# Mixture of experts: order by token count, half-width slots for four experts, 2 MB weight transfers

## The chip, the cores and the metric

The kernel runs on one core of a Trainium2 chip. The metric is the time of one execution on the device, in microseconds (us); lower is better. In the rows PE is the matrix engine (TensorE), PEld its weight loads, DVE the vector engine, ACT the scalar engine, POOL the GpSimd engine and SP the engine that issues the weight transfers; SPq is its queue. 1 MB is 1,048,576 bytes throughout.

## The reference, cut to what matters

The network has two blocks over 256 tokens of width 1024 in fp32. The changed part is the mixture of experts that ends the first block:

```python
def moe_swiglu(h, w_router, w_gate_up, w_down):
    t = h.reshape(-1, D)                                    # 256 x 1024
    logits = (t @ w_router).astype(F32)                     # 8 experts
    top_val, top_idx = lax.top_k(logits, TOP_K)             # 2 of 8
    top_w = jax.nn.softmax(top_val, axis=-1)
    combine = jnp.sum(jax.nn.one_hot(top_idx, N_EXPERTS, dtype=F32) * top_w[..., None], axis=1)
    for e in range(N_EXPERTS):
        gt, up = jnp.split(t @ w_gate_up[e], 2, axis=-1)    # 1024 x 2*3584
        y = (jax.nn.silu(gt) * up) @ w_down[e]              # 3584 x 1024
        out = out + combine[:, e:e + 1].astype(t.dtype) * y
```

With the inputs of the measurement the eight experts get 55, 74, 53, 86, 71, 54, 55 and 64 of the 512 (token, expert) pairs. An expert's weights are 42 MB, all experts' 336 MB.

## The kernel before

**Products.** An fp32 product is made of parts that the matrix engine takes at full rate: x = xH + xL and w = wH + wL, and `mm3` (L185, matmuls at L187 to L189) adds wH xH, wL xH and wH xL. Weights come from DRAM into a ring of raw slots of 1 MB (DMA at L172, on SP's queue), ACT copies the high part wH (L182) and DVE subtracts to get wL (L183), 1024 columns of 128 partitions, half a slot, at a time.

**Routing.** `route` computes logits, ranks and `place`, each token's place among its expert's tokens. The count of the fullest expert goes to a register (`values_load`, L977); if it is over 128 a branch (L872) runs all experts again on the tokens beyond 128.

**Experts.** `experts` takes experts 0 to 7 in this order, each with 128 slots. For a pair of experts `pair` gathers the tokens of both by a product with a one-hot matrix (L998) and makes the parts hH and hL. Each expert has 7 groups of 512 hidden columns. `up` makes the gate and up products of a group (8 blocks of channels, each an `mm3` of a 128x128 stationary block of tokens and 512 weight columns, result `gu`), then silu on ACT (L1086), the product with up on DVE (L1087), four transposes on PE (L192) and the parts aH (ACT) and aL (DVE). `down` adds the group before it into two accumulators `acc` (2 halves x 4 blocks of `mm3`). So an expert has 7 x 2 x 8 x 3 + 7 x 2 x 4 x 3 = 504 of these matmuls. After the last group `scatter` adds the slots' results to the tokens (L1134 to L1136). `first_gates` makes the gates of expert 0's first group for all tokens while the routing still runs.

**Rings.** During the experts `more_raw` lengthens the ring to 12 slots: the 5 slots that all stages share, 5 new ones and 2 in the pair of tiles (`hp`) that the stage before has used for its operand parts. The whole program lies in one `weights` context (`tile_stages`), so the next stage, `mixer_2`, loads into the same 5 slots.

Of the kernel before, what the change touches and what calls it, by code (L numbers as in the profile page):

```python
# [30 lines left out]
RAW = 5  # L31
LEVELS = (64, 32, 16, 8, 4, 2, 1)
# [53 lines left out]
class Net:  # L86
    def __init__(self, ctx, tc, A, out):
# [3 lines left out]
        self.grain = 1024  # columns of weights that are split in one operation  # L91
# [4 lines left out]
        self.turn = 0  # of hp, the one last taken from  # L96
# [32 lines left out]
    def more_raw(self, bufs, more):  # L129
        """Lengthens the ring of bufs raw weights, by more new ones and the two tiles of hp that aren't in use."""  # L130
        was, spare = self.ring, self.hp[1 - self.turn]
        with self.tc.tile_pool(name="more", bufs=more) as pool:
            more_ = lambda n: pool.tile([128, n], F32, name="raw", tag="raw")
            spare_ = [lambda n, tag=tag: spare.tile([128, n], F32, name="raw", tag=tag) for tag in ("hH", "hL")]
            turns = itertools.cycle([more_] * more + [was[0]] * bufs + spare_)
            self.ring = (lambda n: next(turns)(n)), *was[1:]
            yield
        self.ring = was
# [12 lines left out]
    def row(self, ap, pool, name, eng=None, **k):  # L151
        """One row of DRAM on all partitions."""
# [5 lines left out]
    def col(self, ap, pool, name, eng=None):  # L158
        """A row of 1024 in DRAM as [128, chunk]."""
# [4 lines left out]
    def unit(self, srcs, a, b):  # L164
        """The weights of a ring's slot, [128, a, b], and their two exact parts. srcs: (index of the view, DRAM AP)."""
# [14 lines left out]
    def parts(self, H, L, src):  # L180
        """src = H + L, each of 12 significant bits."""
# [12 lines left out]
    def rstd(self, ss, n, width):  # L194
        """ss [128, width] sums of squares -> 1/sqrt(mean + eps)."""
# [5 lines left out]
    def power(self, x):  # L201
        """1/sqrt(x) of x [128, few]."""
# [4 lines left out]
    def squares(self, x, ss, junk=None):  # L207
        """The sum of squares of each row of x [128, <=512] to ss [128, 1]; on VectorE with junk."""
# [6 lines left out]
    def to_T(self, src, t, u, dH, dL, psum):  # L215
        """Half u of the channels of src [128 tokens, 1024] -> parts of the transpose in dH/dL[:, :, t*128:]."""
# [1333 lines left out]
```

## Time and profile before

| | before |
|---|---|
| three runs, median (lowest to highest) | 1872.41 us (1871.2 to 1872.74) |
| profiled execution, span from its first to its last instruction | 1871.3 us |
| PE busy | 1811.4 us, 97% |
| DVE busy | 1477.5 us, 79% |
| ACT busy | 1230.4 us, 66% |
| moved by DMA | 511.36 MB (of 10^6 bytes) |

The profiled execution's only time is its span; it lies 1.1 us under the median of the runs. Busy time is a sum over stages with different limits, so the experts' stage, from about 516 to 1528 us, has to be read by itself.

### The profile page before, as it was taken

To read this page: it belongs to the slowest core of one execution; us is meant where nothing else is said; L and a number is where in the kernel's file an instruction comes from. 1 tells how busy PE (TensorE), PEld (TensorE's weight loads), DVE (VectorE), ACT (ScalarE), POOL (GpSimd) and SP (SyncE) were. 2 spreads that over 40 slices of the span, in tenths; PEclk is the share of its full clock that TensorE was granted. 3 is DMA by queue.
4 is the path that set the end of the run, shared out by engine and by line. 5 is a ranking of instruction groups with operands and counts; after the bars stand their busy time and mean duration, and the time that the engine had idled before them with its cause. 6 is when DMAs were issued, how large, how long until landed. Compare 5 with 4: busy or idle time off the path is not lost. (4 is left out here: it accounts for less than half of the span.)

```text
span 1871.3 us, 23420 instructions
## 1 busy us (share of the span) xinstructions
PE 1811.4 (97%) x8504; PEld 1455.9 (78%) x8504; DVE 1477.5 (79%) x1826; ACT 1230.4 (66%) x1768; POOL 73.1 (4%) x113
## 2 busy tenths in 40 slices
PE   7999999999999999999999999999999979989997
PEld 5767787788778888788787887887887857778886
DVE  4767888676789998898988989988898876575555
ACT  5665444575678777777777777777777766565443
POOL 2002000120100000000000000000000010000001
PEclk9999999999999999999999999999999989999999
DMA  8536899643579999899999999998999935345551
GB/s 250 172 94 232 311 335 328 223 149 113 208 275 364 372 356 370 324 351 365 341 372 346 338 361 356 355 371 301 360 376 341 345 122 169 129 158 191 180 180 45
DMA packets 226299, 511.36 MB, mean 273 GB/s; under 512 B 11301, under 2 KB 37013, under 8 KB 223104
## 3 DMA queue, kind: packets, MB, share of 16 engines
q1 hardware_dynamic: 221872, 501.84, 75.6%
q0 software_dynamic: 2832, 7.09, 1.5%
q8 instruction: 69, 1.13, 0.2%
q10 hardware_dynamic: 1472, 0.86, 0.2%
q14 instruction: 54, 0.44, 0.1%
HBM read 507.10 MB, written 2.65 MB: 272 GB/s over the span
## 5 line engine op out<-in xcount | busy, mean ns | idle before, releaser
L183 DVE TENSOR_TENSOR wL<-raw,wH 128x1024 fp32r<-128x1024 f32 (+1 forms) x1001 | 1072.0, 1115 | 209.3 <-issue 125.7
L182 ACT ACTIVATE wH<-raw 128x1024 fp32r<-128x1024 f32 (+1 forms) x1001 | 912.3, 969 | 242.5 <-PE acc L189 70.1
L187 PE MATMUL gu<-wH,hH 128*128 128x512 f32 x1192 | 467.5, 392 | 2.3 <-ACT hH L1000 2.3
L188 PE MATMUL gu<-wL,hH 128*128 128x512 f32 x1192 | 466.3, 391 | 3.1 <-DVE wL L183 3.0
L189 PE MATMUL gu<-wH,hL 128*128 128x512 f32 x1192 | 465.5, 391 | 0.0
L188 PEld LDWEIGHTS gu<-wL,hH 128*128 128x128 f32 x1192 | 224.4, 188 | 56.4 <-DVE wL L183 5.7
L189 PE MATMUL acc<-wH,aL 128*128 128x512 f32 x664 | 265.5, 400 | 0.0
L187 PEld LDWEIGHTS gu<-wH,hH 128*128 128x128 f32 x1192 | 224.4, 188 | 51.0 <-ACT hH L1000 3.7
L188 PE MATMUL acc<-wL,aH 128*128 128x512 f32 x664 | 263.4, 397 | 0.0
L189 PEld LDWEIGHTS gu<-wH,hL 128*128 128x128 f32 x1192 | 224.2, 188 | 46.6 <-issue 1.1
L187 PE MATMUL acc<-wH,aH 128*128 128x512 f32 x664 | 257.3, 402 | 0.0
L187 PE MATMUL mm<-wH,hH 128*128 128x512 f32 (+1 forms) x384 | 151.7, 396 | 0.8 <-ACT hH L1478 0.5
L188 PE MATMUL mm<-wL,hH 128*128 128x512 f32 (+1 forms) x384 | 150.2, 391 | 0.0
L188 PEld LDWEIGHTS acc<-wL,aH 128*128 128x128 f32 x664 | 124.8, 188 | 32.2 <-DVE wL L183 4.1
L189 PE MATMUL mm<-wH,hL 128*128 128x512 f32 (+1 forms) x384 | 149.4, 390 | 0.0
L187 PEld LDWEIGHTS acc<-wH,aH 128*128 128x128 f32 x664 | 124.9, 188 | 26.5 <-issue 0.5
L189 PEld LDWEIGHTS acc<-wH,aL 128*128 128x128 f32 x664 | 124.8, 188 | 26.5 <-issue 0.5
L182 ACT ACTIVATE aH<-tp 128x512 fp32r<-128x512 f32 (+1 forms) x94 | 51.1, 545 | 120.3 <-PE tp L192 120.2
L187 PEld LDWEIGHTS mm<-wH,hH 128*128 128x128 f32 x384 | 73.2, 191 | 15.3 <-issue 1.7
L188 PEld LDWEIGHTS mm<-wL,hH 128*128 128x128 f32 x384 | 73.2, 191 | 14.5 <-issue 2.7
L189 PEld LDWEIGHTS mm<-wH,hL 128*128 128x128 f32 x384 | 73.2, 191 | 13.5 <-issue 1.7
L1087 DVE SCALAR_TENSOR_TENSOR act<-gu,r_slot,act 128x512 f32<-128x512 f32 x56 | 42.0, 749 | 49.2 <-PE gu L189 49.2
(434 smaller groups left out, 1428.5 us busy)
## 6 DMA issues: line engine op xcount, KB each, us to landing
raw<-in_moe_w_gate_up_dram SPq DMA_DIRECT2D x224, 1024.0 KB, 7.3
raw<-in_moe_w_down_dram SPq DMA_DIRECT2D x112, 1024.0 KB, 6.4
raw<-in_w_ff_dram SPq DMA_DIRECT2D x32, 1024.0 KB, 5.0
raw<-in_w_ada_dram SPq DMA_DIRECT2D x24, 1024.0 KB, 4.9
raw<-in_dense_w_gate_up_dram SPq DMA_DIRECT2D x44, 512.0 KB, 5.2
raw<-in_b_w_in_dram SPq DMA_DIRECT2D x12, 1024.0 KB, 5.1
raw<-in_w_in_dram SPq DMA_DIRECT2D x12, 1024.0 KB, 5.5
raw<-in_dense_w_down_dram SPq DMA_DIRECT2D x11, 1024.0 KB, 5.1
```

What stands on the lines that cost most here:

```text
L182: self.high = self.nc.scalar.activation(H, src, AF.Copy)
L183: self.low = self.nc.vector.tensor_tensor(L, src, H.bitcast(F32), op=OP.subtract)
L187: mm(ps, xH, wH, start=start, stop=False)
L188: mm(ps, xH, wL, start=False, stop=False)
L189: mm(ps, xL, wH, start=False, stop=stop)
L1087: nc.vector.scalar_tensor_tensor(a, ps[1], r, a, op0=OP.mult, op1=OP.mult)
```

## The change

**Order.** After the counts are known, `order` (a function inside `route`) ranks the experts by their count on DVE, expert 0 first whatever it has. SP reads the seven numbers of the others and the fullest count into registers; the weights of turns 1 to 7 are then addressed by register.

**Slots.** Turns 0 to 3 have 128 slots as before. Turns 4 to 7 have 64, and their stationary operand holds the 64 high columns beside the 64 low ones. One 128x512 matmul with wH makes wH xH in the upper half of the result and wH xL in the lower; a second with wL uses the 64 high columns alone (`product`). That is 2 matmuls for 3. The halves of the gate are added by copying the result (ACT, `halves`) and an fp32 product with `fold`, which sums slots i and i+64. The up product is not folded: the four transposes become fp32 products with `fold`, which add the halves as they transpose. The one-hot is written twice, so that the scatter adds the halves.

**Weights.** A transfer fills a slot of 2 MB: 4 blocks of channels x 1024 columns for gate and up (runs of 4 KB in DRAM, before 2 KB), and 16 KB per partition in one run for down (before 4 KB). `wH` and `wL` are made 2048 columns at a time. Groups are taken in steps (0), (1,2), (3,4), (5,6). The ring has 4 slots of 2 MB and the spare `hp` pair (2 x 1 MB), 10 MB in all, before 12 MB.

**Gathers** are made for turns (0), (1,2), (3) and (4 to 7), each ahead of the last `down` of the turn before it. Activations are issued behind the first piece of the `down` before them.

**Fallback.** The branch is taken when a count is over 128, or over 64 in turns 4 to 7. Ranked, the counts above are 55 (expert 0), 86, 74, 71 and 64, 55, 54, 53.

**Contexts.** The experts no longer lie in the shared `weights` context; `mixer_2` and `mlp` open one of their own behind it.

```diff
...
+    def wide_weights(self, slots, high, low, size, spare=None):
...
+            n = 4096 if slots else size
+            slot = lambda: a.tile([128, n], F32, name="raw", tag="raw")
+            turns = [[slot] * (4096 // n)] * max(1, slots)
+            if spare is not None:
+                turns.append([lambda tag=tag: spare.tile([128, size], F32, name="raw", tag=tag) for tag in ("hH", "hL")])
...
+        for make in next(turns):
+            raw = make()
+            n = raw.shape[-1]
+            nc.sync.dma_start(raw.rearrange("p (c b) -> p c b", b=b), src[:, c:c + n // b])
+            for i in range(0, n, size):
+                H = pH.tile([128, size], F32R, name="wH")
+                L = pL.tile([128, size], F32R, name="wL")
+                self.parts(H, L, raw[:, i:i + size])
+                view = lambda x: x.rearrange("p (c b) -> p c b", b=b)
+                yield range(c, c + size // b), view(H), view(L)
+                c += size // b
...
-            with self.more_raw(RAW, 5):
-                self.experts(sb, psum, route, self.cst["iota"], f.x)
...
+            with self.wide_weights(4, 3, 2, 2048, self.hp[1 - self.turn]):
+                self.experts(sb, psum, route, self.cst["iota"], self.cst["iota"], f.x)
+            with self.wide_weights(0, 1, 1, 1024), tc.If(route["most"] > 128):
...
+        fold = sb.tile([128, 128], F32, name="fold")
+        for i in range(2):
+            nc.gpsimd.tensor_tensor(fold[:, i * 64:(i + 1) * 64], ident[:, :64], ident[:, 64:], op=OP.add)
...
+            nc.vector.tensor_scalar(cnt[:, 0:1], cnt[:, 0:1], 1000.0, None, op0=OP.add)
...
+            nc.vector.tensor_scalar(full[:, BIG_TURNS:], full[:, BIG_TURNS:], 64.0, None, op0=OP.add)
+            nc.vector.tensor_reduce(which[:, 0:1], full, axis=AX.X, op=OP.max)
...
+            route["expert"] = [0] + [nc.values_load(whole[0:1, i:i + 1], engines=sp, min_val=0, max_val=NE - 1)
+                                     for i in range(1, NE)]
+            route["most"] = nc.values_load(whole[0:1, 0:1], min_val=0, max_val=T + 64)
...
+                if small:
+                    for x, d in ((H, slice(0, 2)), (L, slice(2, 4))):
+                        v = x[:, k].rearrange("p (e h s) -> p e h s", e=2, h=2)
+                        nc.scalar.activation(v[:, :, 0], o[:, d], AF.Copy, scale=g[:, k:k + 1])
+                        nc.vector.scalar_tensor_tensor(v[:, :, 1], o[:, d], g[:, k:k + 1], v[:, :, 0].bitcast(F32),
+                                                       op0=OP.mult, op1=OP.subtract)
...
+        steps = ((0,), (1, 2), (3, 4), (5, 6))
+        groups = ((0,), (1, 2), (3,), (4, 5, 6, 7))
...
+            c0, n = i * FE + js[0] * 512, len(js) * 512
+            for k0 in range(0, KC, 4096 // n):
+                for ks, H, L in self.pieces(W1[expert(e), :, k0:k0 + 4096 // n, c0:c0 + n], n):
+                    yield [(k0 + k, [(H[:, k - ks[0], d:d + 512], L[:, k - ks[0], d:d + 512]) for d in range(0, n, 512)])
+                           for k in ks]
...
+            if len(x) == 2:
+                self.mm3(ps, *x, H, L, start, stop)
+                return
+            high = lambda: mm(ps, x[0], H, start=start, stop=stop)
+            if start:
+                high()
+            mm(ps[:64], x[0][:, :64], L, start=False, stop=False)
+            if not start:
+                high()
+        def fold(ps):
+            x = sb.tile([128, 512], F32, name="halves", bufs=2)
+            nc.scalar.copy(x, ps)
+            return lambda: mm(ps, route["fold"], x, start=True, stop=True)
...
+                for ws in w1(e, js, i):
+                    for g in range(len(js)):
+                        for k, hl in ws:
+                            product(ps[i][g], [y[:, k] for y in xe], *hl[g], k == 0, k == KC - 1)
+                    while folds:
+                        folds.pop(0)()
+                if small and i == 0:
+                    folds = [fold(p) for p in ps[i]]
...
+                for c in range(4):
+                    if small:
+                        mm(pt[:, c * w:(c + 1) * w], a[:, c::4], route["fold"][:, :w], start=True, stop=True)
+                    else:
+                        self.transpose(pt[:, c * w:(c + 1) * w], a[:, c::4])
+                pt = pt[:, :4 * w].rearrange("p (c s) -> p c s", c=4)
+                if small:
+                    y = sb.tile([128, 4, 128], F32R, name="aH", bufs=2)
+                    self.parts(y[:, :, :64], y[:, :, 64:], pt)
+                    return (y,)
...
+            for ks, H, L in self.pieces(W2[expert(e), j], D):
+                for h in range(2):
+                    d = slice(h * 512, (h + 1) * 512)
+                    for k in ks:
+                        product(acc[h], [y[:, k] for y in a], H[:, k - ks[0], d], L[:, k - ks[0], d],
+                                j == 0 and k == 0, j == steps[-1][-1] and k == 3)
+                yield
...
+            if js == steps[-1] and e + 1 in first:
+                if pend is not None and e not in ohTs:
+                    ohT(e)
+                fetch(first[e + 1])
...
 def tile_stages(net):
+    with net.weights(RAW, 3, 2), net.memory():
+        f = net.first()
+        f = net.dense(f)
+        f = net.hgrn(f)
+    net.moe(f)
     with net.weights(RAW, 3, 2):
-        with net.memory():
-            f = net.first()
-            f = net.dense(f)
-            f = net.hgrn(f)
-        net.moe(f)
         st = net.mixer_2()
         net.mlp(st)
```

SP, the start of the experts' weights, before (`raw` is a ring slot; the brackets name the semaphores that a row waits for):

```order
L172 DMA raw_4423<-in_b_w_out_dram 128x4x512 [waits DMAHW4_49,DVE_49,Activation_49]
L172 DMA raw_4834<-in_moe_w_gate_up_dram 128x4x512 [waits DMAHW5_49,DVE_49,Activation_49]
L172 DMA raw_4854<-in_moe_w_gate_up_dram 128x4x512 [waits DMAHW6_49,DVE_49,Activation_49]
L172 DMA raw_4874<-in_moe_w_gate_up_dram 128x4x512 [waits DMAHW7_49,DVE_49,Activation_49]
L172 DMA raw_4574<-in_moe_w_gate_up_dram 128x4x512 [waits DMASW0_49,DMASW1_49,DVE_49,DMASW2_49,PE_49,DMASW7_49,Activation_49,Pool_49]
```

The same place in the changed kernel, SP:

```order
L192 DMA raw_4423<-in_b_w_out_dram 128x4x512 [waits DMAHW4_49,DVE_49,Activation_49]
L151 DMA raw_4981<-in_moe_w_gate_up_dram 128x2x1024 [waits DVE_49,PE_49]
L151 DMA raw_4586<-in_moe_w_gate_up_dram 128x8x512 [waits DMASW1_49,DMASW0_49,DMASW2_49,DVE_49,DMASW7_49,PE_49,Pool_49]
L151 DMA raw_4713<-in_moe_w_gate_up_dram 128x8x512 [waits DMASW5_49,DMASW6_49,DMASW4_49,DMASW3_49]
L151 DMA raw_4913<-in_moe_w_gate_up_dram 128x4x1024 [waits DMAHW5_49]
```

The first three transfers of before go to shared slots. In the changed kernel the first one, raw_4981, goes to the spare `hp` pair, which out_proj's matmuls of the stage before still read, and raw_4586, which the first gates need, stands behind it.

PE, the gate products of a turn with 64 slots in the changed kernel (`gu0`, its first result), up to the fold:

```order
L1148 MATMUL gu0_8507<-wL_8551,hH_8171 64x512
L1145 MATMUL gu0_8507<-wH_8550,hH_8171 128x512
L1156 MATMUL gu0_8506<-halves_8562,fold_4504 128x512
L1148 MATMUL gu1_8508<-wL_8569,hH_8171 64x512 x2
L1145 MATMUL gu1_8508<-wH_8568,hH_8171 128x512
L1148 MATMUL gu1_8509<-wL_8569,hH_8171 64x512 x2
L1145 MATMUL gu1_8509<-wH_8568,hH_8171 128x512
L1156 MATMUL gu0_8507<-halves_8564,fold_4504 128x512
```

Matmuls of 128 and of 64 stationary columns alternate, and the up products of the next piece (`gu1`) stand between the two folds. Before, three matmuls of 128 columns stand for each block, L187, L188 and L189.

SP, the end of the experts, before:

```order
L172 DMA raw_12603<-in_moe_w_down_dram 128x2x1024 [waits DMAHW1_49,DVE_49]
L172 DMA raw_22118<-in_w_in_2_dram 128x8x16 [waits DMAHW3_49,DMAHW2_49,DVE_49]
L172 DMA raw_22173<-in_w_in_2_dram 128x4x512 [waits DMAHW4_49,DVE_49]
L172 DMA raw_22209<-in_w_in_2_dram 128x4x512 [waits DMAHW5_49,DVE_49]
L172 DMA raw_22273<-in_w_in_2_dram 128x4x512 [waits DMAHW6_49,DVE_49]
L172 DMA raw_22309<-in_w_in_2_dram 128x4x512 [waits DMAHW7_49,DVE_49]
L872 COMPARE_AND_BRANCH
```

and the first weights of `mixer_2` in the changed kernel, SP:

```order
L892 UNCONDITIONAL_BRANCH [waits DMAHW0_49,DMAHW1_49,DMAHW2_49,DMAHW3_49,DMAHW4_49,DMAHW5_49,DMAHW6_49,DMAHW7_49]
L192 DMA raw_20107<-in_w_in_2_dram 128x8x16 [waits Activation_sequencer_49,PE_sequencer_49,Pool_sequencer_49,DVE_sequencer_49,DVE_49,SP_sequencer_49,PE_49,DMAHW3_49,Activation_49,Pool_49]
L192 DMA raw_20162<-in_w_in_2_dram 128x4x512 [waits DMAHW4_49]
L192 DMA raw_20198<-in_w_in_2_dram 128x4x512 [waits DMAHW5_49]
L192 DMA raw_20262<-in_w_in_2_dram 128x4x512 [waits DMAHW6_49]
```

Before, five transfers for `mixer_2` stand ahead of the branch. In the changed kernel they stand behind the branch's block and wait for every engine.

## Rows read from the trace of the kernel before

**Rows 1.** The page, busy time of each engine over the span.

```profile
PE 1811.4 (97%) x8504; PEld 1455.9 (78%) x8504; DVE 1477.5 (79%) x1826; ACT 1230.4 (66%) x1768; POOL 73.1 (4%) x113
```

**Rows 2.** Windows: each engine's busy us (xcount), PEclk (granted clock), DMA share, GB/s.

```profile
500.00:516.00 16.00, 16.00 (x75) 13.08 (x75) 10.87 (x15) 10.00 (x18) 0.00 (x0) 1.00 1.04 397
...
561.00:650.00 89.00, 89.00 (x400) 72.93 (x399) 80.83 (x75) 70.47 (x75) 0.00 (x0) 1.00 1.01 370
...
1041.00:1525.00 484.00, 480.21 (x2154) 389.27 (x2152) 430.29 (x415) 357.34 (x400) 0.00 (x0) 1.00 0.94 339
1525.00:1545.00 20.00, 7.74 (x24) 4.80 (x23) 14.65 (x32) 12.58 (x30) 6.24 (x8) 0.60 0.30 85
```

**Rows 3.** Groups by line and shape, 1041 to 1525: busy, mean | idle before, releasers.

```profile
L183 DVE TENSOR_TENSOR wL<-raw,wH 128x1024 fp32r<-128x1024 f32 x326 | 379.4, 1217 | 13.6 <-issue 10.9 <-PE gu L188 1.4 <-ACT wH L182 1.1
L182 ACT ACTIVATE wH<-raw 128x1024 fp32r<-128x1024 f32 x324 | 318.7, 1051 | 18.5 <-PE gu L189 8.6 <-ACT wH L182 3.4 <-PE acc L189 3.1
...
L1087 DVE SCALAR_TENSOR_TENSOR act<-gu,r_slot,act 128x512 f32<-128x512 f32 x27 | 20.3, 751 | 34.8 <-PE gu L189 34.8
L1086 ACT ACTIVATE act<-gu,r_slot 128x512 f32<-128x512 f32 x27 | 18.6, 690 | 18.8 <-PE gu L189 18.7
L183 DVE TENSOR_TENSOR aL<-tp,aH 128x512 fp32r<-128x512 f32 x27 | 18.4, 683 | 0.0
...
L182 ACT ACTIVATE aH<-tp 128x512 fp32r<-128x512 f32 x27 | 16.1, 597 | 79.6 <-PE tp L192 79.6
```

**Rows 4.** Waits of SP's queue, 1041 to 1525: total us, times, longest.

```profile
SPq L172 <- DVE wL L183: 402.3, 154, 16.5
```

**Rows 5.** Timeline of PE at the experts' start: start, us, engine, line, op.

```profile
513.95 0.39 PE L187 MATMUL gr<-wH,hH 128*128 128x512 f32 x1
...
515.77 0.40 PE L189 MATMUL gr<-wH,hL 128*128 128x512 f32 x1
...
518.29 0.40 PE L187 MATMUL gate<-wH,hH 128*128 128x512 f32 x1
```

**Rows 6.** Two lines of source: L849 (384 fp32 columns), L318 (64), ns min/median/max.

```profile
L849 PE MATMUL skew_ps<-oh_h,cst x6: 482/535/587, 178.8 to 184.4; 33*128 33x384 f32 x6
...
L318 PE MATMUL mem_o<-kvV,mem_pT x8: 217/275/275, 122.3 to 123.0; 128*128 128x64 f32 x8
```

**Rows 7.** One tile, ada_H and ada_L, 2048 columns: ns min/median/max.

```profile
L182 ACT ACTIVATE ada_H<-ada_acc x3: 1902/1912/1920, 216.1 to 329.4; 128x2048 fp32r<-128x2048 f32 x3
L183 DVE TENSOR_TENSOR ada_L<-ada_acc,ada_H x3: 2281/2282/2293, 218.7 to 332.5; 128x2048 fp32r<-128x2048 f32 x3
```

**Rows 8.** Timeline of SP, 470 to 556 and 1495 to 1560: start, us over all xcount.

```profile
471.10 29.37 SPq L172 DMA_DIRECT2D raw<-in_moe_w_gate_up_dram  x8
...
515.97 3.67 SPq L172 DMA_DIRECT2D raw<-in_moe_w_gate_up_dram  x4
...
1505.11 52.33 SPq L172 DMA_DIRECT2D raw<-in_w_in_dram  x9
```

**Rows 9.** The page, DMA issues: KB each, median us from issue to landing.

```profile
raw<-in_w_ada_dram SPq DMA_DIRECT2D x24, 1024.0 KB, 4.9
```

**Rows 10.** The branch (L872) on PE's queue; timeline of PE behind the experts.

```profile
L872 PEldq COMPARE_BRANCH  x1: 3512/3512/3512, 1529.0 to 1529.0; - x1
...
1539.80 1.08 PE L192 MATMUL tp<-cst,y_n 128*128 128x128 f32 x4 [11.15 <-DVE y_n L1379]
...
1541.56 0.80 PE L187 MATMUL mm<-wH,hH 128*128 128x512 f32 x1
```

**Rows 11.** Timeline of PE, two products with 2 stationary columns between ones with 128.

```profile
251.48 0.40 PE L189 MATMUL acc<-wH,aL 128*128 128x512 f32 x1
251.72 0.39 PE L838 MATMUL ada_ps<-ada_H,onesr 128*2 128x512 f32 x1
251.94 0.40 PE L839 MATMUL ada_ps<-ada_L,onesr 128*2 128x512 f32 x1
252.18 0.40 PE L187 MATMUL acc<-wH,aH 128*128 128x512 f32 x1
```

More of the change, by code (lines that the diff above doesn't have):

```diff
@@ L128, in more_raw, with pieces @@
     @contextmanager
[L129 to L136, printed above, removed]
-            yield
-        self.ring = was
+    def wide_weights(self, slots, high, low, size, spare=None):
+        pool = self.tc.tile_pool
+        with pool(name="wide", bufs=max(1, slots)) as a, pool(name="wh", bufs=high) as b, pool(name="wl", bufs=low) as c:
+            n = 4096 if slots else size
[3 more added lines that the diff above has]
+                turns.append([lambda tag=tag: spare.tile([128, size], F32, name="raw", tag=tag) for tag in ("hH", "hL")])
+            self.wide = itertools.cycle(turns), (b, c), size
+            yield
+    def pieces(self, src, b):
+        nc = self.nc
+        turns, (pH, pL), size = self.wide
+        c = 0
+        for make in next(turns):
[9 more added lines that the diff above has]
+                c += size // b
     def h_parts(self, other=True):
@@ L1032, in ohT @@
[L1032 to L1041 removed]
+                for i in range(2 * n):
+                    self.transpose(ps[:, i * 128:(i + 1) * 128], oh[:, i % 2, i0 + i // 2].bitcast(F32))
@@ L1072, in up @@
             for i in range(1 if gates else 0, 2):
-                for k, wH, wL in halves(e, j, i):
-                    self.mm3(ps[i], xH[:, k, s], xL[:, k, s], wH, wL, k == 0, k == KC - 1)
-            high = self.high
-            if j == 0 and e % 2 == 0:
-                by["r"] = by["later"]()
-            a = sb.tile([128, 512], F32, name="act", bufs=2)
-            r = by["r"][:, e % 2:e % 2 + 1]
-            if gates:
-                for i in range(4):
-                    nc.tensor.matmul(ps[0], by["oh"][:, i // 2, 0], gates[i // 2][i % 2], start=i == 0, stop=i == 3)
-                nc.scalar.copy(a, ps[0])
-            else:
-                with self.tc.issue_after(high.ins):
-                    nc.scalar.activation(a, ps[0], AF.Silu, scale=r)
@@ new lines, in up, with activations @@
+                if small and i == 0:
+                    folds = [fold(p) for p in ps[i]]
+            high = self.high
+            if js[0] == 0 and i0 == 0:
+                by["r"] = by["factors"]()
+            r = by["r"][:, i0:i0 + 1]
+            acts = []
+            def activations():
+                for g in range(len(js)):
+                    a = sb.tile([128, 512], F32, name="act", bufs=2)
+                    acts.append(a)
+                    gate, u = ps[0][g], ps[1][g]
+                    if gates:
+                        for i in range(4):
+                            mm(gate, by["oh"][:, i // 2, 0], gates[i // 2][i % 2], start=i == 0, stop=i == 3)
+                        nc.scalar.copy(a, gate)
+                    else:
+                        with self.tc.issue_after(high.ins):
+                            nc.scalar.activation(a, gate, AF.Silu, scale=r)
+                    nc.vector.scalar_tensor_tensor(a, u, r, a, op0=OP.mult, op1=OP.mult)
```

233 lines of the change are left out of this document (142 added, 91 removed).

## The prediction

> **What bounds the kernel now.** The page's busy times come first: PE is busy for 97% of the span [rows 1]. The windows say whether that also holds where the change lies. From 1041 us (expert 3's scatter) to 1525 us (expert 7's) PE is busy 480.2 of 484 us at a granted clock of 1.00; DVE is busy 430.3, ACT 357.3 [rows 2]. So four experts take 484 us, 121 each, and PE is the bound. DVE is close behind with 89%. DMA looks full too (share 1.01, 370 GB/s from 561 to 650 us [rows 2]), and whether it is decides what a faster PE brings. The waits of SP's queue answer that: over the same 484 us it waited 402.3 us for DVE's wL to give back a ring slot [rows 4]. Transfers wait for PE's pace, then, and the high share is queued work. Between 500 and 516 us, with eight transfers issued since 471, DMA moved 397 GB/s, 2.64 us a MB [rows 2, 8]; PE's pace asks for 42 MB in 121 us, 2.88 us a MB. DMA has some 8% in reserve, no more. Neither reserve is as large as the third of the matmuls that turns 4 to 7 lose.
>
> **PE in turns 4 to 7.** Matmuls of 512 columns start 0.228 us apart (eight steps from 513.95 to 515.77 [rows 5]). An expert had 504, about 115 us of its 121. Now it has 336: 77 us. Added are seven folds of 512 fp32 columns and 28 folding transposes of 64. An fp32 matmul stands as two records: 384 columns took 0.535 each and 64 columns started 0.1 apart (eight records from 122.3 to 123.0) [rows 6]. By these a fold is 1.0 to 1.4 us (I take 1.2, as records overlap) and a transpose 0.2, together 8.4 + 5.6 = 14. With 3 to 4 us for scatter and gather PE needs about 95 us an expert, 380 for four, 104 less than now. That would be the gain if nothing else bound.
>
> **DVE in turns 4 to 7.** The subtraction for wL is still made of every weight, and only its pieces change. 1024 columns have a mean of 1.217 us and occupy 379.4/326 = 1.164 [rows 3]; 2048 columns took 2.282 [rows 7], so by the same overlap 2.23. Four experts need 168 of these: 374 us, only 5 under the 379 of now. All else on DVE is 430.3 - 379.4 = 51 us; aL at half its width saves about 7, the gather's separate halves add about 3. Sum: 421 us. In addition DVE now sits out 34.8 us in front of its act [rows 3], because that waits for the last up product with more wL behind it in the same queue. PE's slack made those waits free; a DVE that sets the pace pays some of them. So DVE's bounds are 421 (none) and 456 (all).
>
> **DMA in turns 4 to 7.** 168 MB, of which up to 10 can lie in the ring when the phase begins: 158 x 2.64 = 417 us at the rate of 500 to 516, or 158 x 2.83 = 447 if the 370 GB/s of the middle is all there is [rows 2]. The longer runs can help only here, and no row shows 4 or 16 KB runs alone; as nothing excludes a loss either, I keep 2.64 with these two ends.
>
> **ACT** has 168 copies of 2048 columns at 1.912 [rows 7], by the same overlap 1.85, so 310 us for the 318.7 of now; of the other 39 us aH loses 6 and `halves` adds 28 copies as long as aH's of now, 17. That makes 360 busy, hidden under DVE, unless its waits count (below).
>
> The phase therefore goes from 484 us to DVE's 421 to 456, with DMA beside it at 417 to 447. Two limits this close seldom overlap perfectly, so I take **445**: 39 us saved of PE's 104.
>
> **Turns 0 to 3** keep `mm3`, 128 slots and their count of matmuls, and PE covers DVE and DMA there as it does now; their larger pieces and merged gathers I cost at nothing. If that cover failed, DVE's 35 us of act waits per four experts are the size of it.
>
> **The start.** Before, eight transfers of gate and up weights were issued between 471 and 500.5 us, into shared slots, and the first gate product ran at 518.29 [rows 5, 8]. In the changed order SP's first transfer goes to the `hp` pair, whose reader is out_proj's last matmul at 515.77 [rows 5]; in before the transfers into that pair were issued at 515.97 [rows 8]. Everything behind it on SP's queue waits too, the first gates' 2 MB included. 1 MB landed 4.9 us after its issue on a free queue [rows 9]; the 2 MB behind it need 5.3 more: 526 us. One copy of 1.9 us [rows 7] later the first gate can run, at 528: **+10 us**. Between 516 and 528 PE has the router's products and the first gather chunks, small ones, so nothing fills it. From then DMA must keep up without those 8 MB; gates for all tokens take 11 us for 2 MB, which lets it get ahead. Bounds: 7 (the gathers that moved ahead count) to 15 (one more 2 MB piece is late, 5.3).
>
> **The reads of seven numbers** stand on SP behind fifteen transfers of expert 0, and everything of expert 1 is queued behind them. Eight reads of some half a microsecond are hidden as long as the ring holds weights for 10 MB x 2.88 = 29 us of products; uncovered they would cost 4.
>
> **The end.** Before, `mixer_2`'s first transfers were issued at 1505 [rows 8] and its first product ran at 1541.56, after a stretch in which PE waited 11.15 us for the norm [rows 10]; that wait began at 1528.65, so the product ran 12.9 us behind the experts. Now the transfers are issued when all engines have passed the branch, which held PE's queue for 3.5 us from 1529.0 [rows 10], so some 4 us behind the experts; 1 MB lands 4.9 us later and is split in about 2.4, so the product can start 11 to 14 us behind them. I take **+2 us**, with 0 and 8 as ends (a second MB late at each of two places).
>
> **Sum**, against the profiled span of 1871.3 us, 1.1 under the median of the runs: -39 + 10 + 2 = -27, 1844 us as span, **1845** as a run.
>
> **The rivals.**
>
> *The array empties at each change of width (slower).* In turns 4 to 7 matmuls with 128 and with 64 stationary columns alternate, up to 336 changes an expert. A matmul lasts about 0.39 us and the next starts 0.228 after it, so a full wait would add 0.16: 95 + 54 = 149 us an expert, 597 for four, and 1871 + 113 + 12 = 1996. It becomes the bound above (445/4 - 95)/336 = 0.05 us a change, and the kernel is slower than before from (118 - 95)/336 = 0.07. Against it: between products with 128 stationary columns stand two with 2 columns, and they start 0.24, 0.22, 0.24 us apart, as if nothing had changed [rows 11]. The Trainium skill, "TensorEngine Tiling (Array Packing)", section "Key Properties", says that changing the tiling mode drains the TensorE. By that rule, if a narrower operand is another mode, the time would be this rival's; rows 11 speak against it for 2 columns, and no row shows 64.
>
> *Little gain (about 1867).* ACT and DVE work in order, and ACT now waits 79.6 us for the transposes ahead of aH and 18.8 ahead of silu [rows 3]. If a chain of these waits bound the phase, ACT would need 360 + 98 = 458 us; with DMA at 2.83 us a MB for all 168 MB (the ring never ahead) it is 475. That saves 9 to 26; with start and end at 12 to 18, the run lands between 1858 and 1882. For it speaks that three engines and DMA are within 15% of each other; against it, that a ring of three wH lets ACT run ahead of PE over such a wait.
>
> *PE remains the bound (about 1780).* If longer runs and pieces bring DVE and DMA below 380 us, all 104 come through: 1871 - 104 + 12 = 1779. Rows 7 exclude it unless 2048 columns run faster here than there: 374 for wL alone leaves 6 for all else. The Trainium skill, "DMA: Bandwidth & Descriptors", section "Bandwidth", gives 341 GB/s for a transfer of 1 MB and 425 for one of 16 MB. At 425 the 158 MB would take 390 us as an estimate, still over PE's 380; the trace has 397 with transfers of 1 MB queued [rows 2].
>
> *The branch is taken.* A turn with 64 slots has exactly 64 tokens; one more, and all experts run again: some 900 us more. The counts come from the reference's inputs, so I give it 1 in 100.
>
> **How the numbers follow.** The forecast, 1828 to 1860, has 0.56. A better overlap (DVE at 421 or under, up to PE's bound) has 0.15, of which 0.04 lies near 1780. Little gain has 0.21: 0.06 still faster, 0.07 the same, 0.08 slower. The emptying array has 0.07, the branch 0.01. A measurement tells 0.2%, 3.7 us, from no change. Faster: 0.56 + 0.15 + 0.06 = 0.77; same 0.07; slower 0.08 + 0.07 + 0.01 = 0.16. The range from 1806 (DVE's 421 with the low ends of start and end gives 1817; 11 toward PE's bound) to 1880 leaves out PE's bound and its surroundings (0.06), the array and the branch (0.08) and the edge of little gain (0.03).
>
> **What would show it.** Right: between turn 4's and turn 8's scatter about 445 us, PE near 85% busy and waiting for DVE's wL, wL of 2048 columns at 2.2 to 2.3 us with DVE 95% busy or more, the first gate at 528, `mixer_2`'s first product 14 to 18 us behind the experts. Wrong: starts of L1145 and L1148 further apart than 0.24 us with no wait named (array); DMA's share full with SP no longer waiting for slots, or ACT waiting near 100 us in the phase (little gain); PE still 97% busy there (PE's bound). A granted clock under 1.00 in turns 4 to 7 would also break the sum: between 1525 and 1545, where PE was busy 7.7 of 20 us, it was 0.60 [rows 2].

## The result and the profile after

The changed kernel took 1900.32 us (median of 4 runs, 1897.6 to 1901.02) beside 1872.58 for the one before: a ratio of 1.0144, interval 1.0132 to 1.0157. It is slower by 28 us, 1.4%, where the prediction had 1845 (1806 to 1880), a gain.

The page's busy times of the changed kernel, which answer to [rows 1]:

```profile
PE 1769.0 (93%) x8000; PEld 1349.6 (71%) x8000; DVE 1450.4 (76%) x1524; ACT 1203.7 (63%) x1469; POOL 74.6 (4%) x115
```

Its windows, which answer to [rows 2] (busy us (xcount) of PE, PEld, DVE, ACT, POOL, then granted clock, DMA share, GB/s):

```profile
522.00:528.00 6.00, 2.30 (x10) 2.08 (x10) 2.54 (x11) 0.46 (x1) 0.00 (x0) 0.74 1.04 388
528.00:534.00 6.00, 3.40 (x7) 2.29 (x8) 4.49 (x2) 4.36 (x3) 0.00 (x0) 0.50 1.04 400
...
546.00:552.00 6.00, 4.71 (x24) 4.21 (x24) 3.49 (x9) 3.24 (x7) 0.00 (x0) 0.73 1.05 428
552.00:558.00 6.00, 6.00 (x21) 4.87 (x21) 2.74 (x3) 2.30 (x3) 0.00 (x0) 0.70 0.26 109
...
1073.00:1551.00 478.00, 418.10 (x1623) 273.85 (x1622) 407.87 (x242) 343.19 (x253) 0.00 (x0) 0.98 0.90 341
```

Turns 4 to 7 lie from 1073 to 1551 us. PE is no longer busy throughout (418 of 478 us), but DVE (408) and ACT (343) aren't either, and DMA's share fell from 0.94 to 0.90. No engine is full. The granted clock of these turns is 0.98, a mean of TensorE's two levels (1.2 and 2.4 GHz); before, it was 1.00.

Where the time went is seen best from one event of each turn: the start of the first yH copy of its scatter, read from each trace. The table has it for all kernels of this study, the experiments e1 to e18 included, which are told below. Its columns are the time of turn 0's scatter, and the time from there to turn 3's and from turn 3's to turn 7's (us):

```
kernel            scatter of turn 0   turn 0 to turn 3   turn 3 to turn 7
before                 662.2               377.3               484.4
after                  686.3               386.5               478.3
e1_grain               679.5               390.0               517.1
e2_runahead            685.8               386.5               473.1
e3_nolow               690.5               384.6               470.5
e4_oldrings            668.5               380.7               472.0
e5_ah4                 687.6               386.9               469.7
e6_oldrings_ah4        670.0               380.6               472.1
e7_big8                688.6               380.7               502.6
e8_oldrings_big8       667.9               376.5               496.1
e9_single              668.8               380.7               465.4
e10_single_big8        671.1               376.9               496.3
e11_nolow_ah4          687.9               384.9               445.2
e12_fixed              688.5               387.2               382.6
e13_low3               668.3               381.9               465.4
e14_g2048              672.4               376.0               484.0
e15_low3_g2048         671.8               378.4               483.6
e16_low4               670.1               383.2               465.3
e17_pool1              670.9               380.7               466.7
e18_pool2              668.9               381.8               500.5
```

After against before: +24.1 up to the first scatter, +9.2 in turns 1 to 3, -6.1 in turns 4 to 7. From the last scatter's start to the end of the span both take 347 us. Sum: +27.

The groups of turns 4 to 7 on ACT and DVE answer to [rows 3] (busy, mean | idle just before, releasers):

```profile
L202 ACT ACTIVATE wH<-raw 128x2048 fp32r<-128x2048 f32 x162 | 303.7, 1912 | 49.1 <-PE acc L1145 22.0 <-PE gu L1145 21.1 <-DVE wL L203 5.1
L1155 ACT COPY halves<-gu 128x512 f32<-128x512 f32 x27 | 15.5, 583 | 23.9 <-PE gu L1145 23.8
L202 ACT ACTIVATE aH<-tp 128x256 fp32r<-128x256 f32 x27 | 10.4, 384 | 46.7 <-PE acc L1145 36.0 <-PE tp L1223 10.7
...
L203 DVE TENSOR_TENSOR wL<-raw,wH 128x2048 fp32r<-128x2048 f32 x164 | 369.4, 2286 | 35.7 <-ACT wH L202 28.0 <-PE gu L1148 3.9 <-PE acc L1148 2.4
L1216 DVE SCALAR_TENSOR_TENSOR act<-gu,r_slot,act 128x512 f32<-128x512 f32 x27 | 20.1, 748 | 17.6 <-PE gu L1145 17.6
L203 DVE TENSOR_TENSOR aH<-tp,aH 128x256 fp32r<-128x256 f32 x27 | 11.4, 423 | 15.0 <-ACT aH L202 14.9
```

The durations are as forecast (2.29 for the subtraction). The idle times are not: DVE waits for ACT's wH, ACT waits for PE's results, and PE waits for DVE's wL, where before PE hardly waited. A piece of 1 MB is now 8 matmuls, 1.9 us of PE; before, it was 12. The waits of the same turns (total us, times, longest), the second of which answers to [rows 4]:

```profile
PE gu L1148 <- DVE wL L203: 37.6, 38, 3.5
SPq L151 <- DVE wL L203: 360.4, 84, 8.4
```

So the transfers wait for slots here as they did before, and do not set the pace.

How the three engines share the time shows when turn 7's scatter is followed back through the trace, from each instruction to what released it or to the one before it on its engine. Of the 478 us this chain lies 253 on PE, 167 on DVE and 35 on ACT; the rest is hand-over. In the kernel before, 473 of the 484 us are PE's.

### The profile page after: what moved, and what is told of

The parts are those of the page before. It is cut to its first block, busy times and chain, and to the rows that moved or that the text cites. A ratio compares the mean times of both kernels' runs of the same rounds, so it can differ in the third digit from the quotient of the medians.

```text
span 1898.1 us, 21806 instructions
## 1 busy us (share of the span) xinstructions
PE 1769.0 (93%) x8000; PEld 1349.6 (71%) x8000; DVE 1450.4 (76%) x1524; ACT 1203.7 (63%) x1469; POOL 74.6 (4%) x115
## 5 line engine op out<-in xcount | busy, mean ns | idle before, releaser
L203 DVE TENSOR_TENSOR wL<-raw,wH 128x2048 fp32r<-128x2048 f32 (+2 forms) x665 | 1047.2, 1604 | 259.7 <-issue 93.2
L202 ACT ACTIVATE wH<-raw 128x2048 fp32r<-128x2048 f32 (+2 forms) x665 | 883.8, 1363 | 333.1 <-PE gu L209 105.4
L208 PE MATMUL gu<-wL,hH 128*128 128x512 f32 x744 | 294.0, 395 | 0.2 <-DVE wL L203 0.2
L207 PE MATMUL gu<-wH,hH 128*128 128x512 f32 x744 | 289.2, 396 | 0.2 <-ACT hH L1080 0.2
L208 PE MATMUL acc<-wL,aH 128*128 128x512 f32 x440 | 176.3, 401 | 5.7 <-DVE wL L203 5.7
L209 PE MATMUL acc<-wH,aL 128*128 128x512 f32 x440 | 174.3, 396 | 0.0
L207 PEld LDWEIGHTS gu<-wH,hH 128*128 128x128 f32 x744 | 140.2, 189 | 32.5 <-issue 0.7
L1148 PE MATMUL gu<-wL,hL 128*64 128x512 f32 x224 | 92.0, 431 | 24.5 <-DVE wL L203 22.8
L1148 PE MATMUL gu<-wL,hH 128*64 128x512 f32 x224 | 89.1, 418 | 17.4 <-DVE wL L203 15.5
L1148 PE MATMUL acc<-wL,aH 128*64 128x512 f32 x224 | 91.7, 415 | 13.9 <-DVE wL L203 12.7
```

The costliest lines, as they stand in the source:

```text
L202: self.high = self.nc.scalar.activation(H, src, AF.Copy)
L203: self.low = self.nc.vector.tensor_tensor(L, src, H.bitcast(F32), op=OP.subtract)
L207: mm(ps, xH, wH, start=start, stop=False)
L208: mm(ps, xH, wL, start=False, stop=False)
L209: mm(ps, xL, wH, start=False, stop=stop)
L1148: mm(ps[:64], x[0][:, :64], L, start=False, stop=False)
```

## The experiments

Three kernels (e3, e11 and e12) leave work out, as their expectations say. The letters of the theories hold within one expectation or, where the theory is not named again, within its batch.

**First batch: which link is it?** One with half-size operations in `pieces`:

```diff
-                self.parts(H, L, raw[:, i:i + size])
+                for o in range(0, size, self.grain):
+                    d = slice(o, min(size, o + self.grain))
+                    self.parts(H[:, d], L[:, d], raw[:, i + d.start:i + d.stop])
```

> The changed kernel with the split operations of its 2 MB pieces made 1024 columns at a time (two copies and two subtractions for one each); rings, transfers and slots stay. Theory A, hand-over: in turns 4 to 7 no engine is full, and the time goes where ACT, DVE and PE wait for each other's 1 MB pieces over a ring of three wH and two wL. Then half-size operations hand on earlier: turns 4 to 7 fall from 478 us to 450 to 465, turns 1 to 3 from 129 to about 127 each, the run from 1900 to 1870 to 1885. Theory B, transfers: DMA sets the pace, and the run stays within 3 us of 1900. Theory C, DVE's own work sets it: 168 more operations at 0.07 to 0.1 us more per 2048 columns make it 5 to 15 us slower.

Measured: 1935.89 us (ratio to before 1.0328, 1.03 to 1.0356). All three theories missed by far. In its ACT timeline, the second aH of a step now stands behind one short wH:

```profile
1226.34 0.38 ACT L204 ACTIVATE aH<-tp 128x256 fp32r<-128x256 f32 x1 [2.27 <-PE tp L1225]
1226.62 1.05 ACT L204 ACTIVATE wH<-raw 128x1024 fp32r<-128x1024 f32 x1
1233.83 0.38 ACT L204 ACTIVATE aH<-tp 128x256 fp32r<-128x256 f32 x1 [6.16 <-PE acc L1147]
```

ACT waited 6.2 us for the buffer that down's matmuls still read, and the splitting behind it waited as well. In the changed kernel two wH stand there, and the wait in the same step is 0.94 us. Summed over the phase, ACT's waits for acc ahead of aH are 80.6 us in e1 (1080 to 1540) and 36.0 in the changed kernel. But PE was slow in that very stretch. Its window, and two of down's matmuls there:

```profile
1225.00:1235.00 10.00, 9.72 (x33) 7.06 (x32) 6.00 (x7) 2.51 (x4) 0.00 (x0) 0.66 1.04 416
...
1230.15 0.63 PE L1147 MATMUL acc<-wH,aH 128*128 128x512 f32 x1
1230.58 0.63 PE L1150 MATMUL acc<-wL,aH 128*64 128x512 f32 x1
```

They start 0.43 us apart, where at full clock it is 0.23, so part of the 6.2 us is PE's lower clock. Over turns 4 to 7 the granted clock is 0.94 for the changed kernel's 0.98: 6% of 511 us less 2% of 478 is 21 us, an estimate of the clock's share in the 39 us that these turns lost. The place of aH and the clock were not tried apart.

```diff
-            with self.wide_weights(4, 3, 2, 2048, self.hp[1 - self.turn]):
+            with self.wide_weights(3, 4, 3, 2048, self.hp[1 - self.turn]):
```

> The changed kernel with three slots of 2 MB in place of four, and the SBUF this frees given to a fourth wH and a third wL. Theory A, hand-over: the split may run further ahead of PE, so turns 4 to 7 fall from 478 us to 445 to 460 and the run to 1865 to 1885. Theory B, transfers: the ring falls from 10 to 8 MB, so the run is slower, 1905 to 1925. Theory C, DVE's own work: no change, within 4 us of 1900.

Measured: 1896.95 us, turns 4 to 7 473. These turns gained five us of A's 18 to 33; a ring of 8 MB cost nothing, which speaks against B. By its number C fits (within 4 us of 1900); the next run bears on it.

```diff
-                self.parts(H, L, raw[:, i:i + size])
+                if low:
+                    self.parts(H, L, raw[:, i:i + size])
+                else:
+                    self.high, L = nc.scalar.activation(H, raw[:, i:i + size], AF.Copy), H
```

> The changed kernel without the low parts of the weights in turns 4 to 7: DVE's subtraction is left out there, and the matmuls with wL take wH in its place, so PE has the same matmuls. Theories A and C: without DVE's 369 us PE sets the pace, turns 4 to 7 take 385 to 410 us for 478, the run about 1810 to 1835. Theory B, transfers: 168 MB at 2.64 to 2.8 us each keep the phase at 440 to 475, the run 1862 to 1897.

Measured: 1896.7 us, turns 4 to 7 470. DVE's 369 us were gone and 8 us came back. So DVE's work alone isn't the bound. The time is B's (1862 to 1897), its reason is not: SP's queue waited 388.9 of 460 us for ACT to give slots back (last line below).

```profile
1080.00:1540.00 460.00, 408.40 (x1582) 277.87 (x1580) 46.16 (x76) 332.58 (x249) 0.00 (x0) 0.95 0.91 352
```

That is its window, with DVE 10% busy. The granted clock is 0.95, so that the slower PE took back some 13 us (5% of 460 less 2% of 478, an estimate) of what the run might have shown. Its waits (total us, times, longest) have ACT waiting for acc, which must free aH's buffers, and SP waiting for ACT:

```profile
ACT aH L205 <- PE acc L1148: 77.8, 22, 5.3
...
SPq L151 <- ACT wH L158: 388.9, 91, 9.2
```

```diff
-            with self.wide_weights(4, 3, 2, 2048, self.hp[1 - self.turn]):
+            with self.more_raw(RAW, 3):
...
-    with net.weights(RAW, 3, 2), net.memory():
...
     with net.weights(RAW, 3, 2):
+        with net.memory():
```

> The changed kernel on the rings of before: 1 MB slots shared with the stages around, 10 of them, split 1024 columns at a time, and both ends prefetched as before; order by count, 64 slots and steps of two groups stay. Theory A: the start's 24 us come back (first gate at 518 us, expert 0's scatter at 662 to 666), turns 1 to 3 take 126 us or less, turns 4 to 7 450 to 465 as with the half-size operations, so the run is 1838 to 1860. Theory B, in which long transfers are what feeds the phase: the start comes back, but turns 4 to 7 take 480 us or more, the run 1870 to 1885.

Measured: 1871.1 us (ratio 0.999, 0.9977 to 1.0002). The first gate ran at 518.76. The scatter of turn 3 is at 1049.2, for 1072.8 after and 1039.5 before: the new rings, with their 2 MB transfers and operations of 2048 columns, cost 23.6 us by then. Turns 4 to 7 gained 6 us, not the 13 to 28 of A. The run's time is B's (1870 to 1885), but turns 4 to 7 took 472, not B's 480 or more.

**Second batch: aH's buffers, and what the narrow slots are worth.**

```diff
-                    y = sb.tile([128, 4, 128], F32R, name="aH", bufs=2)
+                    y = sb.tile([128, 4, 128], F32R, name="aH", bufs=4)
```

> The changed kernel with four buffers for aH in place of two, nothing else. A step of two groups makes two aH while the two of the step before are still read by down's matmuls, and ACT, which works in order, waits for them with the next copies of weights behind it. Theory A, that this hand-over holds turns 4 to 7: ACT's waits for acc ahead of aH (36 us of the phase) go, turns 4 to 7 fall from 478 to 440 to 458 us, the run from 1900 to 1862 to 1880. Theory B, that the chain is held elsewhere (wH and wL rings, the act chain at the end of a step, PE's clock after its gaps): within 8 us of 1900.

Measured: 1895.79 us, turns 4 to 7 470: B, the wait is worth 8.6 us in the phase.

The same edit on e4:

> Four buffers for aH, on the rings of before (1 MB slots, both ends prefetched), where two buffers gave 1871. Theory A: 1832 to 1852. Theory B: 1862 to 1875.

Measured: 1872.38 us, B again. On these rings the buffers are worth nothing (472.1 in turns 4 to 7, for 472.0).

```diff
-BIG_TURNS = 4
+BIG_TURNS = 8
-        groups = ((0,), (1, 2), (3,), (4, 5, 6, 7))
+        groups = ((0,), (1, 2), (3, 4), (5, 6), (7,))
```

> The changed kernel with 128 slots in all turns (gathers in pairs), so without the two-matmul products, folds and narrow slots; order, steps of two groups and 2 MB transfers stay. If the narrow slots are worth anything, turns 4 to 7 take 129 us each here as turns 1 to 3 do (515 in all), and the run is 1930 to 1942. If their saving is nil, 478 and 1900. If turns of 128 slots run here as in before (121 each), 484 and 1905 to 1910.

Measured: 1918.23 us, turns 4 to 7 502.6, between the first and the third case.

The same edit on e4:

> As the last, but on the rings of before with 1 MB transfers and both ends prefetched: what is left of the change is the order by count, longer runs and the steps of two groups. If the steps of two groups cost the turns of 128 slots their 2 to 7 us each, 1885 to 1905; if the loss of turns 1 to 3 came from the 2 MB pieces, 1872 to 1880.

Measured: 1891.31 us, turns 4 to 7 496.1. On both rings the narrow slots are worth 24 us in turns 4 to 7 (502.6 to 478.3, 496.1 to 472.0), and the same turns with 128 slots take 12 to 18 us longer than the kernel before. For the whole run the narrow slots are worth less, 18 and 20 us: with 128 slots two gathers lie between the scatters of turns 3 and 7, while the changed kernel has made its last gather by then.

**Third batch: steps of one group, and PE alone.** On the rings of before:

```diff
-        steps = ((0,), (1, 2), (3, 4), (5, 6))
+        steps = tuple((j,) for j in range(7))
```

> The changed kernel on the rings of before (1 MB slots, ten of them) and with steps of one group each, as before; what is left of the change is the order by count, the 64 slots of turns 4 to 7 and the new places of gathers and activations. Theory A, that steps of two groups cost turns of either width (a step's two aH, acts and folds come at once and ACT and DVE stand for PE): expert 0's scatter near 663, turns 1 to 3 377 us as before, turns 4 to 7 450 to 462, the run 1845 to 1858. Theory B, that the steps don't matter: within 6 us of the 1871 that the same rings gave with steps of two.

Measured: 1864.2 us, ratio 0.9955 (0.9938 to 0.9971): faster than both kernels, if by half a percent, with 465 in turns 4 to 7. That is short of A, and about 1 us outside B.

With the edit of e7 on top:

> The same with 128 slots in all turns. Theory A: the kernel of before in another order, 1868 to 1878. Theory B: 1885 to 1895, as with steps of two groups.

Measured: 1892.15 us: B. The 12 us that 128 slots cost in turns 4 to 7 aren't due to the steps. The narrow slots are worth 31 us in these turns here, 28 in the run.

The edits of e3 and e5 together, on the changed kernel's own rings:

> The changed kernel without the low parts of the weights in turns 4 to 7 (DVE's subtraction left out, wH multiplied in wL's place, PE's matmuls as many) and with four buffers for aH. Two buffers gave 470 us for these turns. If ACT's wait for aH's buffers was what kept it from gaining, 400 to 425 us and the run 1830 to 1850; if PE itself with its folds and its clock is the bound, 450 to 470 and 1880 to 1897.

Measured: 1868.54 us, turns 4 to 7 445, between both. Followed back as above, the chain lies 385 of the 445 us on PE: with these two links gone PE is the bound again, at a granted clock of 0.93.

```profile
1080.00:1450.00 370.00, 345.11 (x1331) 237.77 (x1330) 40.03 (x66) 283.01 (x212) 0.00 (x0) 0.93 0.97 380
```

And on those rings, with one slot less and two buffers of aH again:

```diff
-                self.parts(H, L, raw[:, i:i + size])
+                if low:
+                    self.parts(H, L, raw[:, i:i + size])
+                else:
+                    H = L = self.fixed
```

> The changed kernel with the weights of turns 4 to 7 neither split nor used: one fixed tile stands for every wH and wL there, and the transfers run on into slots that nobody reads (three of 2 MB and the spare pair). It measures PE with its folds, acts and scatters alone. By the sums of the rows, matmuls 77, folds 5, folding transposes 13 and scatter 4, 99 us a turn, 395 to 405 us for four, if nothing else slows PE; the transfers, which wait for no one, show what 2 MB pieces can be moved at: 2.64 us a MB by the rows of before, 2.5 if long runs help.

Measured: 1818.91 us, turns 4 to 7 382.6, at a clock of 1.00:

```profile
1080.00:1450.00 370.00, 370.00 (x1558) 266.21 (x1556) 45.05 (x73) 49.13 (x88) 0.00 (x0) 1.00 1.02 412
```

PE needs what the prediction said, 380, all of it on the chain, and 2 MB transfers that wait for no one move 412 GB/s, 2.55 us a MB.

**Fourth batch, on e9: more to run ahead on, or fewer operations.** A third wL buffer (e13), or a third and a fourth (e16), for one raw slot less each:

```diff
+            self.lows = itertools.cycle([was[1][1]] * 2 + [extra] * 1)
...
-            L = pL.tile([128, size], F32R, name="wL")
+            L = (next(self.lows) if self.lows else pL).tile([128, size], F32R, name="wL")
```

> Steps of one group on the rings of before (which gave 1864 us, turns 4 to 7 465), with a third wL buffer for one raw slot less (9 MB). Theory A, DVE has no room to run ahead: it may now stand three pieces ahead of PE when it waits for an up product, and turns 4 to 7 fall to 445 to 458, the run to 1845 to 1857. Theory B, DVE's own busy time (91% of these turns) is the bound: 460 to 466 and 1860 to 1866.

Measured: 1864.76 us, 465.4: B.

One operation of 2048 columns for each slot:

```diff
-            for o in range(0, size, self.grain):
-                d = slice(o, o + self.grain)
-                self.parts(H[:, d], L[:, d], raw[:, d])
+            self.parts(H, L, raw)
```

> Steps of one group on the rings of before, each 1 MB slot split by one operation of 2048 columns on ACT and DVE, not two of 1024. Theory A: hand-over comes later for each piece, so turns 4 to 7 take 465 to 485 and the run 1864 to 1885. Theory B: DVE has 0.1 us less for each slot, 17 us of its busy time in turns 4 to 7, which fall to 448 to 456, the run to 1847 to 1856.

Measured: 1883.08 us, 484 in turns 4 to 7: A. DVE's waits for ACT's wH in the phase are 63.6 us for e9's 26.7. The longest in each group lies behind `halves` (ACT, then DVE):

```profile
1213.04 0.58 ACT L1149 COPY halves<-gu 128x512 f32<-128x512 f32 x1 [2.69 <-PE gu L1139]
...
1215.47 4.67 DVE L197 TENSOR_TENSOR wL<-raw,wH 128x2048 fp32r<-128x2048 f32 x2 [2.39 <-ACT wH L196]
```

The third buffer on top changed nothing:

> Both: third wL buffer and one operation for each slot. Theory A: 450 to 465 in turns 4 to 7, run 1850 to 1865; Theory B: 448 to 456, run 1847 to 1856; both at once: 430 to 445 and 1830 to 1845.

Measured: 1884.03 us, none of the three cases.

> Two more wL buffers for two raw slots less (8 MB). Theory A: 435 to 450 in turns 4 to 7, run 1835 to 1850, unless the shorter ring of transfers takes it back. Theory B: as with steps of one group before, 1860 to 1868.

Measured: 1866.2 us, 465.3: B.

**Fifth batch, on e9: less for DVE.**

```diff
-                self.parts(H[:, d], L[:, d], raw[:, d])
+                self.parts(H[:, d], L[:, d], raw[:, d], nc.gpsimd if i + o in pool else nc.vector)
```

> Steps of one group on the rings of before (1864 us, turns 4 to 7 465), with the last of a group's twelve subtractions of 1024 columns in turns 4 to 7 made by POOL, which the trace of before shows at 1.34 us for 512 columns, so about 2.7 us. Theory B, DVE's busy time is the bound: each of 28 groups is 1.1 us shorter, turns 4 to 7 take 432 to 440, the run 1830 to 1840. Theory A, ACT's places in the chain are the bound: 1860 to 1868. If POOL and DVE slow each other: slower than 1864.

Measured: 1864.65 us, 466.7: A.

> Two of twelve subtractions of a group made by POOL. Theory B: 2.2 us less a group as far as PE's 383 us for the four turns allow, 402 to 420 in turns 4 to 7, the run 1800 to 1820. Theory A: 1860 to 1868. If POOL and DVE slow each other: slower than with one.

Measured: 1900.11 us, the third case. POOL's subtraction took 3.1 us and DVE's mean rose from 1.22 to 1.40.

One group of e9 (DVE, then PE, then ACT) shows what holds these turns:

```profile
1204.75 6.90 DVE L199 TENSOR_TENSOR wL<-raw,wH 128x1024 fp32r<-128x1024 f32 x6 [0.52 <-ACT wH L198]
1212.20 4.84 DVE L199 TENSOR_TENSOR wL<-raw,wH 128x1024 fp32r<-128x1024 f32 x4 [0.55 <-ACT wH L198]
1216.95 0.75 DVE L1212 SCALAR_TENSOR_TENSOR act<-gu,r_slot,act 128x512 f32<-128x512 f32 x1
1217.62 2.35 DVE L199 TENSOR_TENSOR wL<-raw,wH 128x1024 fp32r<-128x1024 f32 x2
1220.38 0.42 DVE L199 TENSOR_TENSOR aH<-tp,aH 128x256 fp32r<-128x256 f32 x1 [0.41 <-ACT aH L198]
1221.33 6.90 DVE L199 TENSOR_TENSOR wL<-raw,wH 128x1024 fp32r<-128x1024 f32 x6 [0.52 <-ACT wH L198]
...
1218.08 1.85 PE L1219 MATMUL tp<-fold,act 128*128 128x64 f32 x8
...
1213.59 3.90 ACT L198 ACTIVATE wH<-raw 128x1024 fp32r<-128x1024 f32 x4
1219.96 0.39 ACT L198 ACTIVATE aH<-tp 128x256 fp32r<-128x256 f32 x1 [2.48 <-PE tp L1219]
1220.25 5.79 ACT L198 ACTIVATE wH<-raw 128x1024 fp32r<-128x1024 f32 x6
```

The reader follows the times from one line to the next. Ten wL end at 1216.95, act follows, then PE makes the folding transposes until 1219.93, then ACT makes aH; only behind it does ACT copy the wH that DVE's next six wL need, which start at 1221.33. That is a loop of 16.6 us through three engines (1204.75 to 1221.33), and 28 such loops make 464 us of the 465. Only two of twelve wL lie outside it, in the gap in which DVE would otherwise wait. e17 took one of these two, so the loop stayed at 16.55 (its act starts at 1202.43 and 1218.98). More wL buffers leave it as it is. Operations of 2048 columns lengthen it, mostly at `halves`: DVE waits 2.39 us behind it in each group, for 0.55 in e9, and 0.68 behind aH, for 0.52. No run moved aH within ACT's queue, which would be the direct test of the loop.

## Why the prediction was wrong

**Turns 4 to 7, the step that failed.** "I take 445" took the phase from the sum of one engine's work, DVE's 421 with some of its waits; 39 us were to be saved, and 6 were (478). The busy times were good: DVE 408, PE 382.6 alone for a forecast of 380, transfers at 2.55 us a MB. What bound was none of them. The rival *little gain* had the mechanism, a chain of waits through ACT and DVE in order, and put it at 458, or 475 with slower transfers. It was set back because a ring of three wH lets ACT run ahead; a fourth wH and a third wL were worth 5 us (e2). Its sign came, ACT idle for 135 us where near 100 were named (127 before, so this sign told little), and the forecast's own did not: DVE was 85% busy, not 95.

Taking DVE's subtraction away (e3) gave 8 us, more buffers 5 to 9 (e2, e5) or none (e6), both the subtraction and aH's buffers 33 (e11), everything that ACT and DVE do to the weights 96 (e12). So no engine alone sets the pace; the chain of the changed kernel, 253 us on PE, 167 on DVE and 35 on ACT, says the same, and in e9 (204, 122 and 100) the links can be read off. In the changed kernel, with two groups to a step, the loop was not taken apart link by link. The clock is a second thread: a granted clock under 1.00 was named as a thing that would break the sum, and it was 0.98 here, 2% of PE's 418 us or some 8 us as an estimate. In e1, e3 and e11 it fell to 0.93 to 0.95, so these runs show less gain, or more loss, than their edits would at the clock of the changed kernel.

That PE's 380 met its forecast is in part luck. A folding transpose took 0.46 us for 0.2 (28 of them, 7 us an expert); against that, a fold took 0.86 us in e12 for 1.2, and from scatter to scatter the phase holds the gate and up products of 27 groups (x27 above), where the sum had 28.

Besides, the same turns with 128 slots are 12 to 18 us slower than before in this program (e7, e8, e10), which no step of the prediction had; one gather more is part of it, the rest is open.

**The start.** The first gate was forecast for 528 and ran at 529.5:

```profile
529.50 1.22 PE L207 MATMUL gate<-wH,hH 128*128 128x512 f32 x2 [2.29 <-ACT wH L202]
531.83 0.79 PE L208 MATMUL gate<-wL,hH 128*128 128x512 f32 x1 [1.11 <-DVE wL L203]
```

The +10 was right there and too small as a whole. It took eight transfers as what lay ready before; two of down's weights followed them:

```profile
501.13 5.80 SPq L172 DMA_DIRECT2D raw<-in_moe_w_down_dram  x2
```

From 522 to 534 PE had 5.7 us of work and its granted clock fell to 0.50; after the next gaps it was 0.73 and 0.70 (the windows above), where before it was 1.00. The rings of before (e4) bring the first scatter from 686.3 to 668.5: 17.8 us, for a term of 10. With operations of half the size alone (e1) it is at 679.5, so about 7 of the 17.8 may be the operations' size. Of the rest, up to the 662.2 of before, the gather of turns 1 and 2 is likely a part, which now stands ahead of that scatter (649.6 to 662.1); that was not tried.

**Turns 0 to 3**, costed at nothing, lost 9.2 us behind the first scatter. The rings account for 5.8 of them (380.7 with e4); the other 3.4 stay open. The gathers do not explain them, as both kernels make two between these scatters (before from 767 and 1013 us, after from 882 and 1015).

**The end**, +2: `mixer_2`'s transfers were issued at 1560.05 and its first product ran 13.4 us behind the experts, for 12.9. The cost is half a microsecond; PE's wait for the norm, as long as in [rows 10], hid the rest:

```profile
1566.99 1.08 PE L212 MATMUL tp<-cst,y_n 128*128 128x128 f32 x4 [11.22 <-DVE y_n L1538]
...
1569.13 0.79 PE L207 MATMUL mm<-wH,hH 128*128 128x512 f32 x1
```

**The other rivals.** The array doesn't empty. The timeline of turn 4:

```profile
1143.22 0.39 PE L1145 MATMUL gu<-wH,hH 128*128 128x512 f32 x1
1143.45 0.40 PE L1148 MATMUL gu<-wL,hH 128*64 128x512 f32 x1
1143.68 0.40 PE L1145 MATMUL gu<-wH,hH 128*128 128x512 f32 x1
1143.92 0.39 PE L1148 MATMUL gu<-wL,hH 128*64 128x512 f32 x1
```

Stationary operands of 128 and 64 columns alternate at 0.23 us, as in [rows 5]. The Trainium skill, "TensorEngine Tiling (Array Packing)", section "Key Properties", has a drain for a change of tiling mode; alternating these two widths here shows none. The branch was not taken: no second pass over the experts stands in the trace. The seven reads held SP for 4 us, from 598.1 to 602.3, as priced uncovered, and no wait in the trace names them.

## What to carry to other kernels

When the bounding engine is relieved by a third and two others stand at 70 to 90%, add up the loop, not the engines: follow one result from engine to engine until it releases the work that began it, and see which operations lie inside. An operation that waits in an in-order queue (aH, halves) holds all that is queued behind it, so its place in that queue can cost more than its length: in e1 ACT waited 6.2 us for an aH of 0.38. When a long wait is found, look at the granted clock of that stretch before giving the queue all of it. What lies ready when a stage begins is part of the stage's time; a ring that is taken anew at the border gives it away, and PE pays once more in clock.

## What was not expected of the hardware

The granted clock of turns 4 to 7 differed between kernels in which PE was about equally busy. In e11 it was 0.93 (the window above, PE busy 345 of 370 us), in e1 0.94 (451 of 511), and in e9 it stayed at 1.00:

```profile
1080.00:1450.00 370.00, 341.63 (x1295) 204.39 (x1295) 336.44 (x323) 284.17 (x334) 0.00 (x0) 1.00 1.00 371
```

These are means of the two levels: in e1's stretch above PE waited 0.45 us for act at 1223.4, began the folding transposes, fell to the lower level before they ended, and ran at it until 1233, with matmuls 0.43 us apart for 0.23. What decides between the levels is not shown here.

POOL's subtraction of 1024 columns took 3.1 us on average in e18 and 3.3 in e17, some 2.6 times DVE's, and slowed DVE beside it (mean 1.22 to 1.24 with one of twelve, 1.40 with two). A folding transpose of 64 fp32 columns took about 0.46 us of PE (eight records in 1.85), for the 0.2 that the forecast took from [rows 6].
